# Layer 1 of a two-layer attention trunk: every third pair of probability chunks combined on VectorE, and the sum of squares as two rounded products

## The chip, the cores and the metric

The kernel runs on one core of one Trainium2 chip. The metric is the device time of one execution in microseconds. One execution was also taken by the hardware profiler; where the text speaks of the trace, it means that one.

## The reference

The input x has 2048 tokens of 1024 features. Layer 0 (a sliding-window attention and a chunked one) is not touched by the change. Layer 1 is a differential attention with 8 heads: two softmaxes over the same values, one subtracted from the other, then a norm over each head's 128 features and a gate.

```python
def differential_attention(q1, q2, k1, k2, v, lam):
    ...
        s1 = jnp.einsum('bqhd,bkhd->bhqk', qb1, k1).astype(jnp.float32) * scale
        s2 = jnp.einsum('bqhd,bkhd->bhqk', qb2, k2).astype(jnp.float32) * scale
        p1 = jax.nn.softmax(jnp.where(mask, s1, NEG_INF), axis=-1)
        p2 = jax.nn.softmax(jnp.where(mask, s2, NEG_INF), axis=-1)
        a = p1 - lam * p2
        return jnp.einsum('bhqk,bkhd->bqhd', a.astype(v.dtype), v)
...
    o = differential_attention(q1, q2, k1, k2, v, lam)
    o = rms_norm(o, subln_g) * (1.0 - lambda_init)
    y = (o.reshape(b, s, C_W) * jax.nn.silu(gate)) @ w_out
    return x + y
```

The mask lets a token see its own chunk of 64 tokens and all earlier ones. All of it is in 4-byte floats.

## The kernel before

The kernel runs layer 0, then the projections of layer 1 (q, k, v into DRAM), then the stage `_mix1`, which holds all that the change touches. `_mix1` starts at 1782 us of the span and lasts to the end, 1085 us.

The 2048 queries are cut into four blocks b of 512, each block into four tiles j of 128. The work goes by (head h, block b), 32 of them: first blocks 0 and 1 of each head in turn, then block 2 for all heads, then block 3.

`scores(h, b, ...)` is the first half of one (h, b). For each tile j and each of the two softmaxes m, the visible keys are cut into chunks of up to 512. For a chunk, TensorE multiplies a high and a low part of q with k into a PSUM bank (tile `cS`, L898 and L899), VectorE takes the row's negated maximum (`cnm`, L902), and ScalarE writes the exponentials to SBUF (`cP`, L905) and adds them up. After both softmaxes of a row of chunks, small instructions (L911 to L917) work out the common scale of each chunk: `cpe` at L914 is a VectorE product of two SBUF tiles with at most 8 columns. Then each pair of chunks is made into one, p1 x c1 + p2 x c2. GpSimd scales p1 (L921). For most pairs GpSimd also scales p2 (L930) and adds the two (L931). For every `COMB`th pair VectorE does the second half in one instruction (L928), after a small product for its scalar (L927); both of its inputs lie in SBUF.

`values(h, b, ...)` is the second half. For each 128 keys, TensorE transposes the combined chunks of the four tiles (`ctr`, L944), ScalarE (two in three, L947) or VectorE (one in three, L949) copies the result to SBUF (`cpt`), and TensorE multiplies it with the values into one PSUM bank (`cO`, L951).

`gate(h, b, O)` ends one (h, b). ScalarE copies the sum out of PSUM (`cot`, L966) and squares it (`csq`, L968); the gate's sigmoid is begun (L970, L971) and GpSimd multiplies by the gate (L972). The rest is put off until the third 128 keys of the next (h, b): a product of the squares with a matrix of ones sums over the 128 features (`cms`, L976), in 4-byte operands; ScalarE takes the logarithm (L977), VectorE adds (L978), ScalarE exponentiates (L979), VectorE multiplies (L980). L978 and L980 read two SBUF tiles each. The result goes to DRAM, or is split at once into a high and a low part for the output projection (`split`, L997 and L998).

Beside this, `gates` (the gate's projection, tile `cG`, first) and `projected` (the output projection, tile `com`, later) yield TensorE work in steps of three products (L214 to L216). `pace` runs `heads` (the scores) ahead of the values by `LAG1` units and mixes in the steps of the side work by `STAGES1`. From the program so recorded, a scheduler in the framework sets the final order of each engine's instructions, by its own estimates of their times. All engines run their instructions in that order.

Buffers that the change touches: the pool `pp` holds the chunks of the first softmax until their transposes are done (20 of 512 columns), and `pt` the transposed chunks until their product (6). Operands of the type `F32R` are 4-byte floats that TensorE multiplies in a rounded form. A high part in that type and the difference to the full value as a low part are the kernel's way to keep accuracy; `self.ones` is of that type, and L976 reads it as plain floats.

Of the kernel before, what the change touches and what calls it, by code (L numbers as in the profile page):

```python
# [10 lines left out]
F32 = mybir.dt.float32  # L11
F32R = mybir.dt.float32r
AF = mybir.ActivationFunctionType
ALU = mybir.AluOpType
# [4 lines left out]
P = 128  # L19
# [4 lines left out]
BLK = NTB * P  # L24
# [7 lines left out]
def f32(ap):  # L32
    return ap.bitcast(F32)
# [52 lines left out]
class Trunk:  # L86
# [1 line left out]
    AHEAD = 2  # L88
    BANKS0, LAG0, SHARE0 = (3, 3, 1, 1), 9, 0.85
    FIN = 18  # L90
    COMB = 5
    BANKS1, LAG1 = (4, 2, 1, 1), (30, 30, 36, 36)
    STAGES1 = ((0, 0), (44, 84), (1088, 520))

# [747 lines left out]
    def _mix1(self, es):  # L842
        nc, tc, a, s = self.nc, self.tc, self.a, self.s1
        n = "c"
        pool = lambda nm, bufs, **kw: es.enter_context(tc.tile_pool(name=n + nm, bufs=bufs, **kw))
# [2 lines left out]
        ld = pool("ld", 2)  # L848
        yp = pool("y", 2 * KT)
        vp = pool("v", 4)  # L850
        pp = pool("pp", 20)
        kp = pool("kp", 4)
        sb = pool("sb", 2)
        NS, NTR, NO, NM = self.BANKS1
# [4 lines left out]
        mm = nc.tensor.matmul  # L859
# [17 lines left out]
        def scores(h, b, q, K, res, then):  # L877
# [4 lines left out]
            for j in range(NTB):  # L882
# [35 lines left out]
                for z, (c, ce) in enumerate(cuts):  # L918
# [3 lines left out]
                    count[0] += 1  # L922
                    if count[0] % self.COMB == 0:
                        c2 = rl[:, 1:2]
# [9 lines left out]
        def values(h, b, res):  # L934
            us = res["u"]
            O = pO.tile([P, BLK], F32, tag="O", name=n + "O")
            nkt = (b + 1) * NTB
            for kt in range(nkt):
                j0 = max(0, kt - b * NTB)
                wd = (NTB - j0) * P  # L940
                tp = ptr.tile([P, 512], F32, tag="tr", name=n + "tr")
                kk = (kt % 4) * P
                for j in range(j0, NTB):
                    nc.tensor.transpose(tp[:, (j - j0) * P:(j - j0 + 1) * P], us[j][kt // 4][:, kk:kk + P], self.ident)  # L944
                T = sb.tile([P, 512], F32, tag="pt", name=n + "pt", bufs=6)
                if kt % 3:
                    nc.scalar.activation(T[:, :wd], tp[:, :wd], AF.Copy)  # L947
                else:
                    nc.vector.tensor_copy(T[:, :wd], tp[:, :wd])  # L949
                v = res["v"][kt // 4][:, kk:kk + P]  # L950
                mm(O[:, j0 * P:], v, T[:, :wd], start=(kt == 0), stop=(kt == nkt - 1), skip_group_check=True)  # L951
                if kt == 2:
                    while normal:
                        normal.pop(0)()
                yield wd / P
            gate(h, b, O)
# [3 lines left out]
        def gate(h, b, O):  # L960

            rows, tok = slice(h * P, (h + 1) * P), slice(b * BLK, (b + 1) * BLK)
            g = sb.tile([P, BLK], F32, tag="g", name=n + "gg")
            nc.sync.dma_start(g, s["g"][rows, tok])
            o = ot.tile([P, BLK], F32, tag="ot", name=n + "ot")
            nc.scalar.activation(o, O, AF.Copy)  # L966
            sq = sb.tile([P, BLK], F32, tag="sq", name=n + "sq", bufs=1)
            nc.scalar.activation(sq, o, AF.Square)  # L968
            sg = sb.tile([P, BLK], F32, tag="sg", name=n + "sg", bufs=1)
            nc.scalar.activation(sg, g, AF.Exp, scale=-1.0)  # L970
            nc.scalar.activation(sg, sg, AF.Ln, bias=self.one)  # L971
            nc.gpsimd.tensor_tensor(o, o, g, ALU.mult)  # L972

            def rest():
                ms = ptr.tile([P, BLK], F32, tag="tr", name=n + "ms")
                mm(ms, f32(self.ones), sq, start=True, stop=True)  # L976
                nc.scalar.activation(sq, ms, AF.Ln, bias=self.eps, scale=1.0 / P)  # L977
                nc.vector.scalar_tensor_tensor(sg, sq, 0.5, sg, ALU.mult, ALU.add)  # L978
                nc.scalar.activation(sg, sg, AF.Exp, scale=-1.0)  # L979
                nc.vector.scalar_tensor_tensor(o, o, self.sub, sg, ALU.mult, ALU.mult)  # L980
                if b == 0 or (h, b) in place:
                    split(h, b, o)
                else:
                    nc.sync.dma_start(s["o"][rows, tok], o)
                ended.add((h, b))

            normal.append(rest)
# [7 lines left out]
        def split(h, b, o):  # L995
            yH, yL = y_tiles(h, b)
            nc.scalar.activation(yH, o, AF.Copy)  # L997
            nc.gpsimd.tensor_tensor(yL, o, f32(yH), ALU.subtract)  # L998
            y[b][h] = yH, yL
# [125 lines left out]
        def heads():  # L1125
# [7 lines left out]
            for (h, b), nxt in zip(order, order[1:] + [None]):  # L1133
                at[0] = b
                after, spare = [None, {}], NB - keys(b)
                new = nxt and nxt[0] != h
                if nxt and not new:
                    after[1] = K

                def then(j, m, z):  # L1140
                    if (j, m, z) == (2, 0, 0) and nxt:
                        after[0] = load_q(*nxt)
                    if (j, z) == (1, 0) and new:
                        for i in range(min(spare, keys(nxt[1]))):
                            after[1][i, m] = load_k(nxt[0], i, m)
                    if j == NTB - 1:
                        if new and z + spare < keys(nxt[1]):
                            after[1][z + spare, m] = load_k(nxt[0], z + spare, m)
                        if m == 0 and z not in V:
                            V[z] = load_v(h, z)  # L1150

                res = {}
                yield from scores(h, b, q, K, res, then)
                res["v"] = [V[z] for z in range(b + 1)]
                if new:
                    V = {}
                queue.append(values(h, b, res))
                q, K = after
# [61 lines left out]
```

## Time and profile before

| | before |
|---|---|
| median of 3 runs | 2870.75 us (2856.9 to 2872.15) |
| profiled execution | 2868.88 us, span 2867.1 us |
| mean granted TensorE clock | 0.982 |
| busy in the span: TensorE, VectorE, ScalarE, GpSimd | 2717.2, 1856.3, 1544.8, 1595.3 us |
| busy from 1782 to 2867 us: TensorE, VectorE, ScalarE, GpSimd | 1028.9, 724.6, 688.8, 791.2 us |

In the profile PE is TensorE (PEld its loading of weights), DVE VectorE, ACT ScalarE, POOL GpSimd. A row of a group gives the line, the engine, the operation, the tiles written and read, the shape and the count; then the busy time in us and the mean of one in ns; then the idle time of the engine ahead of these instructions and what ended it. A row of the timeline gives the start and the duration in us, and in brackets the idle time ahead of it and its releaser. Records of TensorE overlap, since its matmuls are pipelined: what one costs in a dense stretch is the step from its start to the next start.

### The profile page before, as it was taken

The page shows a single profiled execution, that of the slowest core. Times are in us where ns is not written, and L with a number is a line of the kernel's source. Part 1 is how long each engine was busy: PE and PEld are TensorE (multiplying, and loading weights), DVE is VectorE, ACT ScalarE, POOL GpSimd, SP SyncE. Part 2 cuts the span into 40 slices and gives each one's busy share as a digit, 9 for nine tenths or more (in the row PEclk, how much of TensorE's full clock was granted, in tenths as well). Part 3 has the DMA queues.
Part 4 walks back from the last instruction along what each step waited for, and adds up shares of the span by engine and source line. Part 5 has one row for each costly group of instructions (what it writes and reads, how often), then busy time and mean ns, then how long its engine had stood idle before and what let it go on. Part 6 is the DMA issues. An engine that isn't in the chain of part 4 may idle for free.

```text
span 2867.1 us, 43943 instructions
## 1 busy us (share of the span) xinstructions
PE 2717.2 (95%) x13384; PEld 2177.3 (76%) x13384; DVE 1856.3 (65%) x4643; ACT 1544.8 (54%) x4015; POOL 1595.3 (56%) x1740
## 2 busy tenths in 40 slices
PE   7999999998899999899999998999999999899999
PEld 5888888787788888777788887776667777566666
DVE  7752285357788875598708860477777677766761
ACT  4443543367767665343344331577777776656652
POOL 3541251334545354267745650578878787878772
PEclk9999999999999999999999999999999999999999
DMA  5673343738877664567875443887858667354543
GB/s 160 226 239 140 114 142 116 232 107 226 229 188 194 181 180 144 191 219 238 264 245 170 132 145 104 268 244 202 235 171 232 180 199 206 112 171 141 149 137 108
DMA packets 356092, 521.68 MB, mean 182 GB/s; under 512 B 44816, under 2 KB 139792, under 8 KB 355856
## 3 DMA queue, kind: packets, MB, share of 16 engines
q1 hardware_dynamic: 355856, 518.87, 60.5%
q8 instruction: 107, 1.75, 0.3%
q14 instruction: 129, 1.06, 0.1%
HBM read 361.70 MB, written 157.02 MB: 181 GB/s over the span
## 4 chain that ended last, share of the span: by engine, by line
PE 71%; DVE 8%; DMA 7%; ACT 4%; issue 2%; POOL 2%; SPq 1%; DVEq 0%; ACTq 0%; POOLq 0%
PE cO L951 7%; PE p1mm L216 5%; PE p1mm L215 5%; PE p1mm L214 5%; PE cS L898 4%; PE cS L899 4%; PE ctr L944 3%; PE p0mm L214 2%; PE p0mm L216 2%; PE p0mm L215 2%; PE com L214 2%; PE com L215 2%; PE com L216 2%; PE mom L214 2%; PE mom L215 2%
## 5 line engine op out<-in xcount | busy, mean ns | idle before, releaser
L905 ACT ACTIVATE cP<-cS,cnm 128x512 f32<-128x512 f32 (+3 forms) x640 | 397.6, 628 | 191.5 <-DVE cnm L902 170.8
L902 DVE TENSOR_REDUCE cnm<-cS 128x1 f32<-128x512 f32 (+3 forms) x640 | 374.3, 603 | 72.4 <-PE cS L899 65.3
L921 POOL TENSOR_SCALAR cP<-cP,crl,ce 128x512 f32<-128x512 f32 (+3 forms) x288 | 215.8, 762 | 186.9 <-DVE crl L916 99.4
L215 PE MATMUL p1mm<-p1wL,p1hH 128*128 128x512 f32 x768 | 302.3, 394 | 0.4 <-POOL p1wL L310 0.4
L214 PE MATMUL p1mm<-p1wH,p1hH 128*128 128x512 f32 x768 | 301.2, 393 | 0.8 <-ACT p1wH L308 0.8
L216 PE MATMUL p1mm<-p1wH,p1hL 128*128 128x512 f32 x768 | 301.9, 393 | 0.0
L951 PE MATMUL cO<-cpt,cv 128*128 128x512 f32 (+3 forms) x640 | 288.6, 539 | 12.3 <-DVE cpt L949 9.6
L310 POOL TENSOR_TENSOR p0wL<-p0ws,p0wH 128x512 fp32r<-128x512 f32 (+1 forms) x124 | 149.7, 1239 | 265.4 <-ACT p0wH L308 255.8
L931 POOL TENSOR_TENSOR cP<-cP,cP 128x512 f32<-128x512 f32 (+3 forms) x256 | 284.9, 1136 | 1.3
L898 PE MATMUL cS<-ck,cqd 128*128 128x512 f32 (+3 forms) x640 | 263.2, 416 | 18.9 <-ACT cP L905 12.0
L310 POOL TENSOR_TENSOR p1wL<-p1ws,p1wH 128x512 fp32r<-128x512 f32 x128 | 169.7, 1346 | 134.3 <-ACT p1wH L308 128.8
L214 PE MATMUL p0mm<-p0wH,p0hH 128*128 128x512 f32 (+1 forms) x640 | 239.1, 375 | 5.2 <-ACT p0vt L472 3.7
L216 PE MATMUL p0mm<-p0wH,p0hL 128*128 128x512 f32 (+1 forms) x640 | 239.5, 375 | 1.5 <-DVE p0hL L336 1.5
L215 PE MATMUL p0mm<-p0wL,p0hH 128*128 128x512 f32 (+1 forms) x640 | 239.1, 374 | 0.0
L899 PE MATMUL cS<-ck,cql 128*128 128x512 f32 (+3 forms) x640 | 234.0, 370 | 4.0 <-DMA cql<-qL 4.0
L944 PEld LDWEIGHTS ctr<-ident,cP 128*128 128x128 f32 x1088 | 137.6, 142 | 115.0 <-issue 60.9
L930 POOL TENSOR_SCALAR cP<-cP,crl,ce 128x512 f32<-128x512 f32 (+3 forms) x230 | 181.4, 800 | 0.7 <-DVE crl L917 0.7
L944 PE MATMUL ctr<-ident,cP 128*128 128x128 f32 x1088 | 174.7, 275 | 2.8 <-POOL cP L931 2.0
L214 PEld LDWEIGHTS p1mm<-p1wH,p1hH 128*128 128x128 f32 x768 | 144.7, 189 | 29.8 <-ACT p1wH L308 1.0
L215 PEld LDWEIGHTS p1mm<-p1wL,p1hH 128*128 128x128 f32 x768 | 144.7, 188 | 29.6 <-POOL p1wL L310 0.8
L216 PEld LDWEIGHTS p1mm<-p1wH,p1hL 128*128 128x128 f32 x768 | 144.7, 188 | 28.7
L898 PEld LDWEIGHTS cS<-ck,cqd 128*128 128x128 f32 x640 | 123.0, 193 | 49.7 <-ACT cP L905 25.6
(306 smaller groups left out, 7296.2 us busy)
## 6 DMA issues: line engine op xcount, KB each, us to landing
p1ws<-in_od_w_in_dram SPq DMA_DIRECT2D x56, 512.0 KB, 4.4
p0ws<-in_ev_w_in_dram SPq DMA_DIRECT2D x48, 512.0 KB, 4.5
ck<-kH SPq DMA_DIRECT2D x144, 128.0 KB, 3.3
ck<-kL SPq DMA_DIRECT2D x144, 128.0 KB, 3.5
cv<-v SPq DMA_DIRECT2D x72, 256.0 KB, 4.2
cqd<-qH SPq DMA_DIRECT2D x128, 128.0 KB, 4.8
cql<-qL SPq DMA_DIRECT2D x128, 128.0 KB, 4.8
cwH<-wgH SPq DMA_DIRECT2D x64, 256.0 KB, 4.6
```

The lines of the kernel that those rows point to most:

```text
L214: mm(ps, aH, bH, start=first, stop=False)
L215: mm(ps, aH, bL, start=False, stop=False)
L216: mm(ps, aL, bH, start=False, stop=last)
L310: low.tensor_tensor(l[:, :width], ws[:, k, :width], f32(h[:, :width]), ALU.subtract)
L898: mm(ps, qd[:, m, js], kt[:, :wd], start=True, stop=False)
L899: self.anchor = mm(ps, ql[:, m, js], kt[:, :wd], start=False, stop=True).ins
L902: nc.vector.tensor_reduce(nm[:, m, z:z + 1], ps, AX.X, ALU.max, negate=True)
L905: nc.scalar.activation(chunks[z][:, :wd], ps, AF.Exp, bias=nm[:, m, z:z + 1], accum_out=acc)
L921: nc.gpsimd.tensor_scalar(p1, p1, rl[:, 0:1], e1, ALU.mult, ALU.mult)
L931: nc.gpsimd.tensor_tensor(p1, p1, p2, ALU.add)
L944: nc.tensor.transpose(tp[:, (j - j0) * P:(j - j0 + 1) * P], us[j][kt // 4][:, kk:kk + P], self.ident)
L951: mm(O[:, j0 * P:], v, T[:, :wd], start=(kt == 0), stop=(kt == nkt - 1), skip_group_check=True)
```

## The change

Three edits. `COMB` goes from 5 to 3, so that VectorE does the second half of every third pair (106 of the 320) and no longer of every fifth (64). The squares are split: ScalarE copies them into the rounded type (`csH`), VectorE subtracts that from the squares (`csL`), and the one product of plain floats becomes two of rounded ones that add up in the same PSUM bank. For the room of the two new tiles `pp` loses one buffer and `pt` one. The lines below L971 move down by up to five: `csH` is at L971, `csL` at L972, the two products are at L980 and L981, and L978, L980 and L1077 of before become L983, L985 and L1082.

```diff
-    COMB = 5
+    COMB = 3
...
-        pp = pool("pp", 20)
+        pp = pool("pp", 19)
...
-                T = sb.tile([P, 512], F32, tag="pt", name=n + "pt", bufs=6)
+                T = sb.tile([P, 512], F32, tag="pt", name=n + "pt", bufs=5)
...
             sq = sb.tile([P, BLK], F32, tag="sq", name=n + "sq", bufs=1)
             nc.scalar.activation(sq, o, AF.Square)
+            sH = sb.tile([P, BLK], F32R, tag="sH", name=n + "sH", bufs=1)
+            sL = sb.tile([P, BLK], F32R, tag="sL", name=n + "sL", bufs=1)
+            nc.scalar.activation(sH, sq, AF.Copy)
+            nc.vector.tensor_tensor(sL, sq, f32(sH), ALU.subtract)
...
             def rest():
                 ms = ptr.tile([P, BLK], F32, tag="tr", name=n + "ms")
-                mm(ms, f32(self.ones), sq, start=True, stop=True)
+                mm(ms, self.ones, sH, start=True, stop=False)
+                mm(ms, self.ones, sL, start=False, stop=True)
```

TensorE's order around the product of the squares of the last (h, b) but one, before and after. The row is the operation, the tiles and the size written.

```order
L951 MATMUL cO<-cpt,cv 128x512 x2
L976 MATMUL cms<-csq,ones 128x512
L951 MATMUL cO<-cpt,cv 128x512
L944 MATMUL ctr<-ident,cP_32130 128x128
L944 MATMUL ctr<-ident,cP_32319 128x128
```

```order
L951 MATMUL cO<-cpt,cv 128x512 x2
L944 MATMUL ctr<-ident,cP_32499 128x128
L944 MATMUL ctr<-ident,cP_32630 128x128
L944 MATMUL ctr<-ident,cP_32775 128x128
L980 MATMUL cms<-csH,ones 128x512
L981 MATMUL cms<-csL,ones 128x512
L951 MATMUL cO<-cpt,cv 128x512
```

The two products stand together, three transposes later than the one did.

VectorE's order in the last row of chunks of the stage, before and after (`cla` and `ce` are the sums and scales of the chunks, `cxr` the residual of the output projection):

```order
L914 TENSOR_TENSOR cpe<-ce,cla 128x8
L915 TENSOR_REDUCE cl<-cpe 128x2
L916 RECIPROCAL crl<-cl 128x2
L917 TENSOR_SCALAR crl<-crl,nlam 128x1
L927 TENSOR_SCALAR cc_33233<-ce,crl 128x1
L928 SCALAR_TENSOR_TENSOR cP_33179<-cP_33212,cc_33233,cP_33179 128x512
L1077 TENSOR_TENSOR cxr<-com,cxr 128x512
L949 COPY cpt<-ctr 128x512
L978 SCALAR_TENSOR_TENSOR csg<-csq,csg 128x512
```

```order
L914 TENSOR_TENSOR cpe<-ce,cla 128x8
L915 TENSOR_REDUCE cl<-cpe 128x2
L916 RECIPROCAL crl<-cl 128x2
L917 TENSOR_SCALAR crl<-crl,nlam 128x1
L927 TENSOR_SCALAR cc_33419<-ce,crl 128x1
L928 SCALAR_TENSOR_TENSOR cP_33351<-cP_33388,cc_33419,cP_33351 128x512
L972 TENSOR_TENSOR csL<-csq,csH 128x512
L1082 TENSOR_TENSOR cxr<-com,cxr 128x512
L949 COPY cpt<-ctr 128x512
L983 SCALAR_TENSOR_TENSOR csg<-csq,csg 128x512
```

The subtraction `csL` comes right behind a combination.

GpSimd's order for one row of four pairs of the last (h, b), before and after:

```order
L921 TENSOR_SCALAR cP_32902<-cP_32902,crl,ce 128x512
L921 TENSOR_SCALAR cP_32922<-cP_32922,crl,ce 128x512
L921 TENSOR_SCALAR cP_32928<-cP_32928,crl,ce 128x512
L921 TENSOR_SCALAR cP_32946<-cP_32946,crl,ce 128x256
L930 TENSOR_SCALAR cP_32955<-cP_32955,crl,ce 128x512
L930 TENSOR_SCALAR cP_32978<-cP_32978,crl,ce 128x512
L930 TENSOR_SCALAR cP_32996<-cP_32996,crl,ce 128x256
L931 TENSOR_TENSOR cP_32902<-cP_32902,cP_32955 128x512
L931 TENSOR_TENSOR cP_32928<-cP_32928,cP_32978 128x512
L931 TENSOR_TENSOR cP_32946<-cP_32946,cP_32996 128x256
```

```order
L921 TENSOR_SCALAR cP_33089<-cP_33089,crl,ce 128x512
L921 TENSOR_SCALAR cP_33109<-cP_33109,crl,ce 128x512
L921 TENSOR_SCALAR cP_33115<-cP_33115,crl,ce 128x512
L921 TENSOR_SCALAR cP_33133<-cP_33133,crl,ce 128x256
L930 TENSOR_SCALAR cP_33159<-cP_33159,crl,ce 128x512
L930 TENSOR_SCALAR cP_33165<-cP_33165,crl,ce 128x512
L931 TENSOR_TENSOR cP_33109<-cP_33109,cP_33159 128x512
L931 TENSOR_TENSOR cP_33115<-cP_33115,cP_33165 128x512
```

Ten instructions became eight: two pairs of this row are now VectorE's, not one.

## The prediction

> **What bounds the kernel now.** I read the totals and the chain on the page first.
>
> ```profile
> PE 2717.2 (95%) x13384; PEld 2177.3 (76%) x13384; DVE 1856.3 (65%) x4643; ACT 1544.8 (54%) x4015; POOL 1595.3 (56%) x1740
> ...
> PE 71%; DVE 8%; DMA 7%; ACT 4%; issue 2%; POOL 2%; SPq 1%; DVEq 0%; ACTq 0%; POOLq 0%
> ```
>
> TensorE carries 71% of the chain that ends last. The edit touches layer 1's attention alone, from 1782 us on, so I cut the busy time by stretch (PE, PEld, DVE, ACT, POOL, then the granted clock):
>
> ```profile
> 1782.00:2867.00 1085.00, 1028.93 (x4608) 754.73 (x4608) 724.59 (x1778) 688.82 (x1928) 791.18 (x896) 0.97 0.63 184
> ...
> 2200.00:2400.00 200.00, 199.89 (x924) 147.14 (x923) 143.88 (x355) 141.68 (x401) 159.75 (x179) 1.00 0.69 201
> 2400.00:2500.00 100.00, 87.09 (x378) 60.66 (x377) 75.37 (x148) 63.67 (x176) 86.19 (x93) 0.93 0.45 127
> 2500.00:2600.00 100.00, 96.40 (x428) 70.35 (x427) 66.04 (x147) 59.13 (x165) 72.55 (x82) 0.98 0.55 166
> 2600.00:2700.00 100.00, 92.51 (x401) 64.94 (x399) 71.44 (x139) 67.01 (x181) 86.92 (x92) 0.97 0.47 137
> 2700.00:2800.00 100.00, 97.50 (x432) 71.38 (x431) 62.24 (x146) 58.17 (x160) 71.88 (x83) 0.97 0.49 150
> ```
>
> In these 1085 us TensorE stands still for 1085 - 1029 = 56 us. The rest of the text is about two things: work taken off TensorE, and whether those 56 us grow or shrink. Who ends them is in TensorE's waits from 1700 us on (us in total, times, longest):
>
> ```profile
> PE cS L898 <- ACT cP L905: 12.0, 10, 3.4
> PE cO L951 <- DVE cpt L949: 9.6, 4, 7.2
> PE com L214 <- DVE cxr L1077: 5.4, 4, 2.1
> PE cG L216 <- DMA cwL<-wgL: 5.0, 1, 5.0
> ...
> PE com L216 <- POOL cy L998: 2.5, 1, 2.5
> PE cO L951 <- ACT cpt L947: 2.3, 1, 2.3
> PE ctr L944 <- POOL cP L931: 2.0, 3, 1.0
> ```
>
> VectorE ends 9.6 + 5.4 us directly. The 12.0 us behind the exponentials are mostly its too, since the exponentials wait for its maxima (first row of the next fence). GpSimd ends only 4.5 us, though it is the busiest of the three helpers.
>
> **The pairs that move from GpSimd to VectorE.** There are 320 pairs of chunks in layer 1: 64 were VectorE's (every fifth), 106 will be (every third), so 42 move.
>
> ```profile
> L905 ACT ACTIVATE cP<-cS,cnm 128x512 f32<-128x512 f32 (+3 forms) x640 | 397.6, 628 | 191.5 <-DVE cnm L902 170.8 <-PE ctr L944 6.4 <-POOL cP L930 5.3
> ...
> L931 POOL TENSOR_TENSOR cP<-cP,cP 128x512 f32<-128x512 f32 (+3 forms) x256 | 284.9, 1136 | 1.3
> ...
> L930 POOL TENSOR_SCALAR cP<-cP,crl,ce 128x512 f32<-128x512 f32 (+3 forms) x230 | 181.4, 800 | 0.7 <-DVE crl L917 0.7
> ...
> L928 DVE SCALAR_TENSOR_TENSOR cP<-cP,cc,cP 128x512 f32<-128x512 f32 (+3 forms) x58 | 63.8, 1100 | 19.1 <-POOL cP L921 18.1 <-DMA cwL<-wgL 0.5
> ...
> L978 DVE SCALAR_TENSOR_TENSOR csg<-csq,csg 128x512 f32<-128x512 f32 x32 | 27.9, 873 | 28.6 <-ACT csq L977 28.4 <-ACT csg L971 0.2
> ...
> L968 ACT ACTIVATE csq<-cot 128x512 f32<-128x512 f32 x32 | 20.4, 639 | 0.1
> ...
> L927 DVE TENSOR_SCALAR cc<-ce,crl 128x1 f32<-128x1 f32 x58 | 12.0, 207 | 1.3
> ```
>
> GpSimd loses 42 x (0.80 + 1.14) = 81 us of 791. VectorE gains 42 x (1.10 + 0.21) = 55 us, and 42 times it also waits for the scaling at L921 (18.1 us over 58, so 0.3 each, 13 us); behind it in VectorE's queue stand the maxima, and behind those the exponentials and the next scores. The saving on GpSimd is off the path: of TensorE's 4.5 us behind it I take back a tenth, 0.5 us (ends: 0 and 4.5).
>
> **The split of the squares.** The copy to sH is a ScalarE pass like the square, 32 x 0.64 = 20 us on top of 689. ScalarE spends 170.8 us before exponentials waiting for VectorE, which covers it; without that cover the 20 us would press on the scores, so its ends are 0 and a few us, and I take 0. The subtraction into sL is a VectorE instruction with two SBUF inputs of 128x512; its nearest row is L978, 0.87 each, 28 us. VectorE thus goes from 725 to 725 + 55 + 28 = 808 us, and its idle share from 33% to 26% (with the 13 us of waiting, 24%).
>
> On TensorE one product of 4-byte operands becomes two rounded ones. Busy times overlap there, so I take steps between starts:
>
> ```profile
> 1841.10 1.02 PE L976 MATMUL cms<-csq,ones 128*128 128x512 f32 x2
> 1841.56 0.80 PE L214 MATMUL cG<-p1hH,cwH 128*128 128x512 f32 x1
> 1842.20 0.40 PE L215 MATMUL cG<-p1hL,cwH 128*128 128x512 f32 x1
> 1842.43 0.39 PE L216 MATMUL cG<-p1hH,cwL 128*128 128x512 f32 x1
> ```
>
> A rounded 512-column product steps by 0.23 (1842.20 to 1842.43). From 1841.10 to 1842.20 stand the old product and one rounded one, so the old one takes 1.10 - 0.23 = 0.87. Two rounded ones take 0.46: 0.41 saved, 32 times, 13.2 us. That is on the engine that bounds; ends: 13.2 where TensorE never waits (2200 to 2400), nothing where the saved time only becomes waiting. TensorE is busy for 95% of the stage: I take 12.5.
>
> At the very end the product itself is waited for:
>
> ```profile
> 2826.21 0.63 ACT L968 ACTIVATE csq<-cot 128x512 f32<-128x512 f32 x1
> ...
> 2826.89 1.13 PE L976 MATMUL cms<-csq,ones 128*128 128x512 f32 x2 [1.35 <-ACT csq L968]
> ...
> 2832.82 1.28 POOL L998 TENSOR_TENSOR cyk<-cot,cyk 128x512 fp32r<-128x512 f32 x1
> ...
> 2836.04 0.39 PE L214 MATMUL com<-p1hH,cyk 128*128 128x512 f32 x1
> ```
>
> TensorE's queue stands for 1.35 us behind the square; now the copy (0.64) comes between: +0.7. The subtraction (0.87) delays the rest of this chain, less 0.41; its last product was ready at 2834.10 for a use at 2836.04, 1.9 us of room, enough for about 1.1 us. Elsewhere the order puts the two products after the transposes of the next block, and I charge nothing; price if a product came too early: its chain is 0.64 + 0.87 = 1.5 us longer, at each of 32 places.
>
> **The smaller pools.** Exponentials wait 6.4 us for a chunk's last transpose (L905's row): one buffer in 20 less, a third of a us. Ends 0 and 6.4, taken as 0. The one buffer less of the transposed chunks takes away waiting room of the copies alone; L947 and L949 stand behind transposes, so 0, at most another 2.3, all that TensorE waits for L947's copies.
>
> **VectorE's longer stalls.** This is the open term.
>
> ```profile
> L914 DVE TENSOR_TENSOR cpe<-ce,cla x96: 144/166/9348, 1802.1 to 2790.8; 128x4 f32<-128x4 f32 x32, 128x6 f32<-128x6 f32 x32, 128x8 f32<-128x8 f32 x32
> ...
> 2475.61 9.35 DVE L914 TENSOR_TENSOR cpe<-ce,cla 128x8 f32<-128x8 f32 x1
> ...
> 2477.54 3.73 POOL L931 TENSOR_TENSOR cP<-cP,cP 128x512 f32<-128x512 f32 x3
> ...
> 2486.76 2.08 PE L951 MATMUL cO<-cpt,cv 128*128 128x512 f32 x2 [7.18 <-DVE cpt L949]
> ...
> 2663.93 7.88 DVE L928 SCALAR_TENSOR_TENSOR cP<-cP,cc,cP 128x256 f32<-128x256 f32 x1
> ...
> 2673.33 0.80 PE L898 MATMUL cS<-ck,cqd 128*128 128x512 f32 x1 [3.17 <-ACT cP L905]
> ```
>
> An 8-column instruction that takes 0.166 in the median took 9.35 us while GpSimd ran back to back, and TensorE stood 7.18 us; a combination took 7.88 and cost 3.17. Both instructions read two SBUF tiles. Such instructions number 96 + 64 + 32 + 32 = 224 now (L914, L928, L978, L980) and 224 + 42 + 32 = 298 then, 1.33 times; GpSimd's load falls to 0.90. Product 1.20: the 10.4 us become 12.4, +2. Ends: -10.4 (no such stall) and +10.4 (twice as many). What else VectorE ends, 9.6 + 5.4 + 12.0 - 10.4 = 16.6 us, I let grow as the inverse of its idle share, 33/26 = 1.27: +4.5; ends 0 and, doubled, +16.6.
>
> The Trainium skill's page "SBUF — State Buffer", section "Who interferes with whom", says that a VectorE instruction with two SBUF inputs and a GpSimd instruction that reads SBUF exclude each other for a whole instruction. By that rule a stall would end with one GpSimd instruction, here 1.3 us, the two long ones would not exist, and the sum would lack its +2. The trace agrees on who collides and not on how long: 9.35 us reach over the three GpSimd additions of the row above and more.
>
> **Sum.** -12.5 - 0.5 + 0.7 + 2 + 4.5 = -5.8 us. The profiled execution took 2868.9 (span 2867.1), 1.9 below the median of 2870.75; 2868.9 - 5.8 = 2863.
>
> **The rivals.** (1) *VectorE's stalls take over: slower.* With 74 more two-source instructions, long stalls that reach TensorE at 7.2 us each: three more (21.6) in place of the +2, and the other waits doubled (16.6 for 4.5) give -5.8 + 19.6 + 12.1 = +26, 2895. It decides from four more stalls of that size on, or two with the waits doubled. For it: VectorE's waits are already the largest group. Against: GpSimd's bursts are shorter; the stall needs a full burst. (2) *GpSimd was the hidden brake: faster.* TensorE idles 12.9 and 7.5 us in the stretches where GpSimd is busy for 86 and 87 of 100, and 3.6 and 2.5 where it is busy for 72. If the two heavy stretches became like the light ones, 14 us come back, beside the 12.5 and without VectorE's terms: -26, 2843. Against: at 2200 to 2400 GpSimd is at 80% and TensorE waits for 0.1. (3) *The saving is swallowed*: the freed 13 us become waiting, 2868.9 + 0.7 + 2 = 2872. In these stretches with waits it may, at 2200 to 2400 it can't.
>
> **How the numbers follow.** A measurement of this kernel can tell about 0.5% (14 us) from no change. My forecast: 0.38; (1) 0.20; (2) 0.30; (3) 0.12. My forecast's own range is 2852 to 2875. Of its 0.38, 0.05 lies below 2856 and 0.01 above 2885; (2) is mostly below (0.27), (1) mostly above (0.17). Faster 0.32, same 0.50, slower 0.18. The range for 8 in 10 reaches from (2)'s 2840 to 2890, inside (1).
>
> **What would show it.** Right: two rounded products per block at steps of 0.23; TensorE's busy time in the stage down by some 8 to 13 us; GpSimd's down by 80; VectorE's up by 80; TensorE's waits for VectorE and the exponentials 3 to 10 us up. Wrong: more VectorE instructions over 5 us with TensorE's waits behind them (1); the 56 us of idle down by 10 or more (2); a wait of TensorE for csL in many blocks.

## The result, and the profile after

The changed kernel takes 2855.0 us in the median of 9 runs (2846.5 to 2862.0), the kernel before 2870.1 in the same session (9 runs, 2856.9 to 2877.0). The ratio is 0.9945 with a 95% interval of 0.9925 to 0.9966: 15 us faster. The forecast was 2863 in a range of 2840 to 2890.

The page after, totals and chain:

```profile
PE 2705.2 (95%) x13384; PEld 2175.9 (76%) x13384; DVE 1890.9 (66%) x4757; ACT 1557.2 (55%) x4047; POOL 1548.9 (54%) x1656
...
PE 67%; DVE 10%; DMA 7%; ACT 4%; POOL 3%; issue 3%; SPq 1%; DVEq 0%; ACTq 0%; POOLq 0%
```

The profiled execution took 2848.2 us, 20.7 less than the one before, but 7.4 of that lie ahead of the stage, in code that didn't change: the stage begins at 1774.6 us, not 1782.0. Over all profiles of this study that start lies between 1774.6 and 1784.3. Two single traces can therefore only be compared stage by stage. The stage after, in the same columns as before:

```profile
1774.60:2846.40 1071.80, 1018.17 (x4608) 754.89 (x4608) 759.50 (x1892) 701.50 (x1960) 747.02 (x812) 0.97 0.64 186
```

It is some 13 us shorter. TensorE's busy time fell by 10.8 us, VectorE's rose by 35, GpSimd's fell by 44. The idle part of TensorE is 53.6 us, before it was 56.1. Its waits have other names now:

```profile
PE cS L898 <- ACT cP L905: 11.9, 14, 2.6
PE cG L214 <- DMA cwH<-wgH: 9.4, 3, 6.8
PE com L214 <- DVE cxr L1082: 4.5, 3, 2.5
PE cO L951 <- DVE cpt L949: 4.4, 7, 1.3
...
PE ctr L944 <- POOL cP L931: 2.7, 3, 1.5
PE cms L980 <- ACT csH L971: 2.4, 2, 2.0
```

The waits for VectorE and for the exponentials fell from 27.0 us to 20.8, with more work on VectorE. Waits for transfers rose in their place. VectorE's two-input instructions after:

```profile
L914 DVE TENSOR_TENSOR cpe<-ce,cla x96: 144/166/2278, 1796.0 to 2768.7; 128x4 f32<-128x4 f32 x32, 128x6 f32<-128x6 f32 x32, 128x8 f32<-128x8 f32 x32
L928 DVE SCALAR_TENSOR_TENSOR cP<-cP,cc,cP x98: 325/984/4887, 1798.0 to 2771.8; 128x512 f32<-128x512 f32 x58, 128x128 f32<-128x128 f32 x18, 128x256 f32<-128x256 f32 x11, 128x384 f32<-128x384 f32 x11
L972 DVE TENSOR_TENSOR csL<-csq,csH x32: 670/732/3176, 1828.1 to 2805.1; 128x512 fp32r<-128x512 f32 x32
```

The longest L914 takes 2.28 us and no longer 9.35.

To compare the experiments, I use three numbers of each trace's stage. *Work*: the steps that TensorE's matmuls need when nothing is waited for, added up (0.226 us for a rounded product of 512 columns, 0.44 for each of the two passes of a plain one, 0.107 for a transpose, narrower ones in proportion). The passes of plain products step by 0.43 in the traces, so 0.44 is a little much: by 0.43 every work would be some 6 us lower, every standing as much higher, and the split would take 13.0 us off the work, not 13.7. *Standing*: the time by which matmuls start later than these steps allow (the expectations call it TensorE's idle time). *Long*: VectorE instructions of over 2 us in the stage that read two SBUF tiles.

Standing is larger than the idle time on the page for two reasons. Overlapping records hide small gaps there. And TensorE's clock is not always granted in full: before, the trace has ten stretches of 3.4 to 13.7 us at half clock in this stage, together 61 us, and each has a wait of TensorE of over 1 us in it or less than 3 us ahead of it. The longest goes with the wait of 7.18 us that the prediction shows. Here are this stretch (the clock is the third number from the end) and, from an undisturbed one, two passes like those that took 2.08 us behind that wait:

```profile
2478.10:2491.70 13.60, 6.42 (x14) 3.05 (x13) 9.19 (x9) 2.23 (x4) 12.75 (x14) 0.50 0.28 77
...
1839.81 1.02 PE L951 MATMUL cO<-cpt,cv 128*128 128x512 f32 x2
```

At half clock a rounded product of 512 columns steps by 0.427 us and not 0.226. TensorE is busy for 45 of the 61 us, so I estimate that 22 us of the standing are slow work and not waiting. A long wait is thus paid twice, and a few long waits more or fewer move TensorE's busy time too.

Before: work 981.4, standing 94.5, long 11. After: work 967.7, standing 94.2, long 4. So by the two profiles the whole gain of the stage is the two rounded products, and nothing else moved. The experiments show that this reading is wrong.

### The profile page after: what moved, and what is told of

Same layout as the page of the kernel before. It is cut to its first block, busy times and chain, and to the rows that moved or that the text cites. A ratio compares the mean times of both kernels' runs of the same rounds, so it can differ in the third digit from the quotient of the medians.

```text
span 2846.4 us, 43958 instructions
## 1 busy us (share of the span) xinstructions
PE 2705.2 (95%) x13384; PEld 2175.9 (76%) x13384; DVE 1890.9 (66%) x4757; ACT 1557.2 (55%) x4047; POOL 1548.9 (54%) x1656
## 4 chain that ended last, share of the span: by engine, by line
PE 67%; DVE 10%; DMA 7%; ACT 4%; POOL 3%; issue 3%; SPq 1%; DVEq 0%; ACTq 0%; POOLq 0%
PE cO L951 7%; PE p1mm L214 4%; PE p1mm L216 4%; PE p1mm L215 4%; PE cS L898 3%; PE ctr L944 3%; PE cS L899 3%; PE p0mm L214 2%; PE p0mm L215 2%; PE p0mm L216 2%; PE mom L214 2%; PE mom L216 2%; PE mom L215 2%; PE com L214 2%; PE com L215 2%
## 5 line engine op out<-in xcount | busy, mean ns | idle before, releaser
L921 POOL TENSOR_SCALAR cP<-cP,crl,ce 128x512 f32<-128x512 f32 (+3 forms) x288 | 221.1, 781 | 207.2 <-DVE crl L916 78.5
L931 POOL TENSOR_TENSOR cP<-cP,cP 128x512 f32<-128x512 f32 (+1 forms) x214 | 254.5, 1208 | 2.0
L930 POOL TENSOR_SCALAR cP<-cP,crl,ce 128x512 f32<-128x512 f32 (+3 forms) x190 | 156.9, 836 | 0.0
```

The costliest lines, as they stand in the source:

```text
L921: nc.gpsimd.tensor_scalar(p1, p1, rl[:, 0:1], e1, ALU.mult, ALU.mult)
L931: nc.gpsimd.tensor_tensor(p1, p1, p2, ALU.add)
```

## The experiments

Each kernel was timed beside the kernel before on the same chip; the ratios are to that. Every edit also changes the order that the scheduler sets. By tiles and sizes, TensorE's order leaves that of before after 35 of 4608 matmuls in the pairs alone, after 615 with L914 on GpSimd, and after 1557 with the smaller pools alone. So an edit can also act through the order, and no run holds the order fixed.

### The two halves of the change apart

The split alone, with its smaller pools, is the changed kernel with one line put back:

```diff
-    COMB = 3
+    COMB = 5
```

> The split of the squares alone (and the smaller pools); every fifth pair stays VectorE's. Theory A (the time follows TensorE's work, the helpers' load is covered): 13 us faster than before, 2857, TensorE's work in the stage down by 13 us and its idle time unchanged. Rival B (part of the gain is GpSimd's relief by the pairs): less than 13, about 2862 to 2866, since VectorE and ScalarE get more work and GpSimd keeps its own. Rival C (the subtraction on VectorE is what helps or harms by stalls): idle time changes by over 5 us.

Measured: 2876.2 us, ratio 1.0035 (1.0021 to 1.0050), 10 us *slower*. Theory A falls, and so does rival B, for neither has a loss; rival C's change of the idle time is there (68.5 us on the page, before 56.1). The work did go down to 967.7, but standing rose to 114.2, with 14 long instructions. VectorE's groups there:

```profile
L914 DVE TENSOR_TENSOR cpe<-ce,cla 128x4 f32<-128x4 f32 (+2 forms) x96 | 61.4, 640 | 33.6 <-ACT ce L913 31.4 <-ACT cP L905 1.8
...
L972 DVE TENSOR_TENSOR csL<-csq,csH 128x512 fp32r<-128x512 f32 x32 | 44.0, 1374 | 9.7 <-ACT csH L971 9.5
```

csL was to take 0.87 us and takes 1.37. Its longest case, from the timeline of VectorE, GpSimd and TensorE in the same kernel:

```profile
2526.59 5.81 DVE L972 TENSOR_TENSOR csL<-csq,csH 128x512 fp32r<-128x512 f32 x1
2532.32 0.15 DVE L914 TENSOR_TENSOR cpe<-ce,cla 128x8 f32<-128x8 f32 x1
...
2527.10 1.29 POOL L931 TENSOR_TENSOR cP<-cP,cP 128x512 f32<-128x512 f32 x1
2528.34 1.30 POOL L976 TENSOR_TENSOR cot<-cot,cgg 128x512 f32<-128x512 f32 x1
2529.59 2.26 POOL L931 TENSOR_TENSOR cP<-cP,cP 128x512 f32<-128x512 f32 x2
2533.08 1.52 POOL L921 TENSOR_SCALAR cP<-cP,crl,ce 128x512 f32<-128x512 f32 x2 [1.23 <-DVE crl L916]
...
2534.03 0.50 PE L214 MATMUL com<-p1hH,cy 128*128 128x512 f32 x1 [2.10 <-DVE cxr L1082]
2543.43 0.50 PE L898 MATMUL cS<-ck,cqd 128*128 128x512 f32 x1 [3.61 <-ACT cP L905]
```

csL starts at 2526.59 while GpSimd runs without a gap, each record beginning before the last one ends, and it ends at 2532.40, just after GpSimd's burst ends at 2531.85. Then GpSimd itself waits 1.23 us for VectorE's scale, and TensorE 2.10 for the residual that stands behind csL. The 3.61 us follow another such stall, a combination of 4.54 us at 2538.08.

The pairs alone are the kernel before with one line of the change:

```diff
-    COMB = 5
+    COMB = 3
```

> Every third pair on VectorE alone; one plain product, the old pools. Theory A: no change, 2870 within 4 us, with 50 us more on VectorE and 75 us less on GpSimd. Rival B (GpSimd was the hidden brake): 8 to 14 us faster, 2856 to 2862, TensorE's idle time in the stage down by that much. Rival D (VectorE's load costs): 5 to 10 us slower, 2875 to 2880.

Measured: 2852.9 us, ratio 0.9957 (0.9941 to 0.9973), 12 us faster with the work unchanged at 981.4. Standing fell to 79.7. Of the long instructions one is left. TensorE's waits for the exponentials and for VectorE's copies are smaller than before (12.0 and 9.6 us), the one for the residual is not (5.4):

```profile
L914 DVE TENSOR_TENSOR cpe<-ce,cla x96: 144/166/2172, 1798.0 to 2769.5; 128x4 f32<-128x4 f32 x32, 128x6 f32<-128x6 f32 x32, 128x8 f32<-128x8 f32 x32
L928 DVE SCALAR_TENSOR_TENSOR cP<-cP,cc,cP x98: 339/1002/1654, 1800.0 to 2771.8; 128x512 f32<-128x512 f32 x58, 128x128 f32<-128x128 f32 x18, 128x256 f32<-128x256 f32 x11, 128x384 f32<-128x384 f32 x11
...
PE cS L898 <- ACT cP L905: 8.4, 10, 2.3
PE com L214 <- DVE cxr L1077: 6.5, 2, 5.1
...
PE cO L951 <- DVE cpt L949: 4.8, 8, 1.1
```

So rival B's size is right. The stage's row tells why VectorE's load didn't cost: it grew by only 6 us (724.6 to 730.4) although 42 combinations came to it, since much of the time that its instructions had stood was gone: L914 took 58.6 us in all before and takes 32.0 here.

```profile
1775.80:2845.80 1070.00, 1025.47 (x4608) 752.86 (x4608) 730.39 (x1860) 688.06 (x1928) 738.08 (x812) 0.98 0.64 186
```

The pools alone, all else as before:

```diff
-        pp = pool("pp", 20)
-                T = sb.tile([P, 512], F32, tag="pt", name=n + "pt", bufs=6)
+        pp = pool("pp", 19)
+                T = sb.tile([P, 512], F32, tag="pt", name=n + "pt", bufs=5)
```

> Only the two pools smaller by one buffer each, all else as before. Theory A: no change, 2870 within 3 us. A rival in which the buffers are what limits the scores' run ahead: 3 to 8 us slower, with more waiting of the exponentials for transposes than the 6.4 us of before.

Measured: 2864.9, ratio 1.0000 (0.9985 to 1.0015). They cost nothing that can be measured. The trace holds a warning, though: here too there are 14 long instructions, 12 of them at L914, which takes 69.9 us in all against 58.6 before, and yet standing is only some 97 us, before it was 94.5. So the number of long instructions alone doesn't set the time; it matters whether TensorE comes to wait behind them. Its order, too, differs from that of before, without a change of the time.

### Is TensorE's work paid in full?

The kernel before with the product over the squares twice:

```diff
-                mm(ms, f32(self.ones), sq, start=True, stop=True)
-                nc.scalar.activation(sq, ms, AF.Ln, bias=self.eps, scale=1.0 / P)
+                mm(ms, f32(self.ones), sq, start=True, stop=False)
+                mm(ms, f32(self.ones), sq, start=False, stop=True)
+                nc.scalar.activation(sq, ms, AF.Ln, bias=self.eps, scale=0.5 / P)
```

> As before, but the plain product over the squares is done twice into the same bank and the sum halved by the scale of the logarithm: 32 times 0.87 us = 28 us more work on TensorE, nothing more on other engines. Theory A: 26 to 28 us slower, 2896 to 2898, TensorE's idle time in the stage unchanged. Rival (freed or added work is swallowed by the waiting): at most half, 2884 or less.

Measured: 2888.3, ratio 1.0078 (1.0061 to 1.0096): 17 to 28 us slower. Work 1009.5, standing 93.0, so 28 us more work. Added work is paid for the most part; "at most half" (1.0049) is excluded. That work which comes off is repaid doesn't follow, and the split alone shows the contrary.

### Which standing, and by whom

Theory L, named in these expectations, says that VectorE instructions with two SBUF inputs are locked out while GpSimd runs back to back, and that TensorE's standing follows; rival G says that GpSimd's load as such is the brake. Three kernels ask which it is. First the product at L914 on GpSimd, all else as before:

```diff
-                    nc.vector.tensor_tensor(pe, e[:, :, :nb], la[:, :, :nb], ALU.mult)
+                    nc.gpsimd.tensor_tensor(pe, e[:, :, :nb], la[:, :, :nb], ALU.mult)
```

> As before, but the small product at L914 (two SBUF tiles of up to 8 columns) is made on GpSimd; nothing else changes. Theory L: VectorE loses the instruction that has the most long stalls (44 us over its 96 undisturbed durations), TensorE's idle time falls by 8 to 15 us, 2851 to 2858. Rival G (GpSimd's load as such is the brake): GpSimd gets 96 more instructions, so no gain or slower, 2866 to 2875.

Measured: 2854.6, ratio 0.9947 (0.9927 to 0.9966), 15 us faster. One moved line, 96 instructions of at most 8 columns, does as much as the whole change. On GpSimd and in the stage:

```profile
L914 POOL TENSOR_TENSOR cpe<-ce,cla 128x4 f32<-128x4 f32 (+2 forms) x96 | 21.3, 222 | 83.8 <-ACT ce L913 83.7
...
1784.20:2852.80 1068.60, 1019.21 (x4608) 747.82 (x4608) 667.60 (x1682) 689.52 (x1928) 809.96 (x992) 0.99 0.65 187
```

GpSimd is busier than before (810 us against 791), VectorE less by 57, long instructions 3, standing 77.9. The half-clock stretches shrink from 61 us to 31, so some 11 of the 16.6 us less standing are, by the same estimate, work that no longer runs slowly. Rival G, that GpSimd's load as such is the brake, falls: here its load went up and the time down.

Then every second pair, all else as before:

```diff
-    COMB = 5
+    COMB = 2
```

> As the pairs alone, but every second pair (160 of 320) on VectorE: 54 more than with every third, about 70 us more on VectorE and 100 us less on GpSimd. Theory L: the long stalls are already gone with every third, so within 5 us of the pairs alone, 2848 to 2858. Rival G: GpSimd's relief goes on paying, 2843 or less. Rival V (VectorE's load takes over): 2860 or more.

Measured: 2851.8, ratio 0.9945 (0.9925 to 0.9966). GpSimd's busy time in the stage is down to 663 us, 75 below the pairs alone, for no measurable gain; one long instruction, standing 85.5. Theory L fits: the long instructions were already gone. But VectorE's busy time rose by 32 us to 762 in this trace, so a gain from GpSimd's relief and a loss from VectorE's load that cancel are not excluded.

Third, in the split alone, VectorE's subtraction replaced by an instruction of one SBUF input:

```diff
-            sL = sb.tile([P, BLK], F32R, tag="sL", name=n + "sL", bufs=1)
-            nc.vector.tensor_tensor(sL, sq, f32(sH), ALU.subtract)
-                mm(ms, self.ones, sL, start=False, stop=True)
+            sL = small("sL")
+            nc.vector.tensor_reduce(sL, f32(sH), AX.X, ALU.max)
+                mm(ms, self.ones, sH, start=False, stop=True)
```

> As the split alone (every fifth pair on VectorE), but VectorE's subtraction of two SBUF tiles is replaced by a maximum over the 512 columns of csH, one SBUF input and about the same length (0.68 us), and the second product reads csH again with the sum halved: the low part of the squares is left out. TensorE, ScalarE and VectorE keep the split's load. Theory L (two-input VectorE instructions are locked out while GpSimd runs back to back, and TensorE's idle time follows): the split alone's idle of 114 us in the stage goes back to 92 to 100, and with 13 us less work the time is 2853 to 2860. Rival W (the added load of VectorE and ScalarE costs by itself): 2870 or more, as the split alone.

Measured: 2865.8, ratio 0.9987 (0.9974 to 1.0001). It is faster than the split alone by 0.0048, about 14 us, but it misses the forecast of 2853 to 2860. The instruction itself no longer stands:

```profile
L972 DVE TENSOR_REDUCE csL<-csH x32: 618/677/687, 1834.0 to 2827.0; 128x1 f32<-128x512 f32 x32
```

Its longest takes 0.687 us, against 5.81. But long instructions are still 14, six of them now at L983, and standing is 107.3: of the 14 to 22 us that theory L wanted off the standing, 7 came. Rival W's 2870 isn't reached either. It isn't isolated to the two inputs alone, for here the second product doesn't wait for VectorE either.

Last, the changed kernel with L914 on GpSimd, by the same line as above:

> The changed kernel with the product at L914 on GpSimd. Theory L: L914's remaining 22 us of standing disappear from VectorE, the stalls of csL and of the combinations stay: 3 to 8 us faster than the changed kernel, about 0.991 of before. Rival G: not faster than the changed kernel.

Measured: 2845.5, ratio 0.9916 (0.9888 to 0.9944), the fastest of all; standing 87.8, long 2. The changed kernel had 0.9945 in its own session, so about 8 us less by the ratios, but the upper end of the one interval lies above the lower end of the other.

### What the split costs

The split alone, csL on GpSimd:

```diff
-            nc.vector.tensor_tensor(sL, sq, f32(sH), ALU.subtract)
+            nc.gpsimd.tensor_tensor(sL, sq, f32(sH), ALU.subtract)
```

> The split alone (every fifth pair on VectorE), with its subtraction csL on GpSimd: 32 x 1.3 = 41 us more on GpSimd, 32 two-input instructions fewer on VectorE. Theory L (standing of two-input instructions is the cost): the split alone was 1.0035 of before; without csL's standing (23 us) and its turn on VectorE it comes to 0.995 to 0.999, TensorE's idle in the stage under 104 us. Rival G (GpSimd's load is the brake): slower than the split alone, 1.005 or more. Rival A2 (ScalarE's extra pass is what costs): stays at 1.0035.

Measured: 2879.8, ratio 1.0041 (1.0024 to 1.0057); theory L's number is missed, and rival A2's, no change against the split alone, is met. With csL on GpSimd its unbroken runs got longer (49 of over 8 us in the stage, 44 in the split alone), and the other instructions stood more: long instructions 24 in place of 14, standing 121.0, L914 74 us in place of 61:

```profile
L914 DVE TENSOR_TENSOR cpe<-ce,cla x96: 145/200/4698, 1798.0 to 2798.0; 128x4 f32<-128x4 f32 x32, 128x6 f32<-128x6 f32 x32, 128x8 f32<-128x8 f32 x32
L972 POOL TENSOR_TENSOR csL<-csq,csH x32: 1266/1280/1738, 1830.7 to 2835.7; 128x512 fp32r<-128x512 f32 x32
```

The remaining three fill a table of the two halves and the place of L914. Their edits are those shown: the split alone with L914 on GpSimd,

> The split alone with the product at L914 on GpSimd, csL on VectorE. Theory L: the split saves TensorE 13 us also without the pairs, if the other two-input instruction is out of the way: 0.991 to 0.994 of before (before with L914 on GpSimd was 0.9947). Rival (the split costs by its load wherever the others stand): 0.996 or more.

the pairs alone with L914 on GpSimd,

> The pairs alone (every third on VectorE), with L914 on GpSimd. Theory L: both remove the same standing, so they don't add up: 0.992 to 0.995 of before, within 4 us of either alone. Rival G: the pairs' relief of GpSimd adds to it, 0.990 or less.

and the changed kernel with both L914 and csL there.

> The changed kernel with L914 and csL on GpSimd. Theory L: only the combinations, L983 and L985 can stand; TensorE's idle under 80 us, 0.988 to 0.991 of before, the fastest so far. Rival G: GpSimd's 41 us more cost, 0.993 or more.

Measured: 2863.8 us, ratio 0.9985 (0.9970 to 1.0000); 2851.3, 0.9937 (0.9921 to 0.9954); 2853.5, 0.9944 (0.9925 to 0.9963). The second is as theory L had it: the pairs and L914's move don't add up. The first and the third miss it, and there the rivals' forecasts came out: 0.996 or more for a split that costs by its load wherever the others stand, 0.993 or more for GpSimd's added 41 us. csL on GpSimd in the last one brought nothing or cost a little.

| ratio to before | L914 on VectorE | L914 on GpSimd |
|---|---|---|
| neither half | 1 | 0.9947 |
| pairs | 0.9957 | 0.9937 |
| split | 1.0035 | 0.9985 |
| both (the change) | 0.9945 | 0.9916 |

| stage | work | standing | long |
|---|---|---|---|
| before | 981.4 | 94.5 | 11 |
| pairs | 981.4 | 79.7 | 1 |
| smaller pools | 981.4 | about 97 | 14 |
| split | 967.7 | 114.2 | 14 |
| both (the change) | 967.7 | 94.2 | 4 |
| L914 on GpSimd | 981.4 | 77.9 | 3 |
| pairs, L914 on GpSimd | 981.4 | 76.3 | 1 |
| split, L914 on GpSimd | 967.7 | 101.4 | 3 |
| both, L914 on GpSimd | 967.7 | 87.8 | 2 |

Against the row that differs by the split and its smaller pools, the split adds 20, 14, 24 and 12 us of standing, and it takes 13.7 off the work. Without the pairs it costs 0.0035 and 0.0038, outside the intervals; with them it gives 0.0012 and 0.0021, inside. So the change's gain is that of the pairs, and the split is about neutral beside them. Put the other way round, the pairs are worth 0.0043 alone and 0.0090 on top of the split: the halves do not add up. Why the split's standing stays even where long stalls are gone isn't settled. By the releasers in the traces, TensorE's standing behind ScalarE grew with the split in all four pairs of rows (24 to 33, 17 to 25, 21 to 25, 20 to 34 us). That could be ScalarE's extra pass, but the smaller pools alone, without that pass, have 31 us there. No run took the pass away alone.

## Why the prediction was near, and which steps failed

The number was 8 us off, and two large errors cancelled in it. That it came so near is luck: the split was forecast as a gain and alone it is a loss, the pairs were forecast as a loss and alone they are the gain.

- *The price of the two products* (0.41 us less, 32 times): right as work, 13 to 14 us. *"That is on the engine that bounds"*, taken at 12.5 us: wrong. Alone the split lost 10 us, since standing grew by 20. Rival (3), which said that the saving would be swallowed and had 0.12, was the nearest for this half.
- *"The saving on GpSimd is off the path"*, 0.5 us, and *+4.5 for VectorE's load*: wrong in sign; both together with the stalls were priced at +6 for the whole change, and the pairs alone gave -12. Rival (2) had the size (-14) and one of its two stretches: with the pairs alone TensorE's idle time from 2400 to 2500 us fell from 12.9 to 6.2, but from 2600 to 2700 only from 7.5 to 6.5. Its agent is not borne out: GpSimd's busy time rose with L914's move while the time fell. The two-input instructions of VectorE that stand behind GpSimd's bursts fit the runs better, but theory L met only four of its eight forecasts.
- *The load of the helpers*: GpSimd's busy time was to fall by 80 us and VectorE's to rise by 80; they fell by 44 and rose by 35. One reason for GpSimd is that the means were taken over all widths: of the 40 combinations that L928's main group gained (58 to 98), only 15 have 512 columns and 14 have 128. On VectorE the standing that left hides part of the load.
- *The waits of TensorE for VectorE and the exponentials*, 3 to 10 us up: they fell by 6.
- *The stalls, 1.33 times the instructions by 0.90 of the load, +2*: the term that failed by its form. Long ones went from 11 to 1 with the pairs and to 4 with the change. I took the chance of standing as proportional to GpSimd's load. The load fell to 0.94, GpSimd's unbroken runs of over 8 us went from 43 to 28 with the pairs and to 31 with the change, and in the row of the order shown two instructions in ten are gone. That the lengths of its runs decide fits these numbers, but no run varied them alone.
- *csL by its nearest row, 0.87*: 0.99 in the change, 1.37 in the split alone.
- *ScalarE's pass costs 0*: not shown, and open, as said below the last table.
- *The end of the kernel, +0.7*: right; TensorE waits 2.01 us there and not 1.35:

```profile
2805.08 0.80 PE L980 MATMUL cms<-csH,ones 128*128 128x512 f32 x1 [2.01 <-ACT csH L971]
```

- *The pools, 0*: right, though the exponentials wait more for transposes:

```profile
L905 ACT ACTIVATE cP<-cS,cnm 128x512 f32<-128x512 f32 (+3 forms) x640 | 398.1, 628 | 202.3 <-DVE cnm L902 161.7 <-PE ctr L944 15.4 <-POOL cP L930 9.1
```

- *Rival (1)*, more stalls, did not happen in the change, but it did in the split alone: with csL added and GpSimd's bursts unshortened, it has 14 long ones and lost 10 us. The smaller pools alone have as many and lost nothing.

## What to carry to other kernels

When one row of a group has a mean several times its median (L914: 0.61 us against 0.166), look at the tail before the busy time: here moving one such tiny instruction to GpSimd gained as much as the whole change. Then check that the bottleneck waits behind it, for a long tail alone need not cost (the smaller pools). Two edits in one change have to be costed, and if possible run, apart; the traces of before and after alone told a clean and wrong story here. Work taken off the busiest engine is a gain only if what replaces it doesn't delay those who feed it.

## What the runs showed of the hardware

A VectorE instruction with two SBUF inputs can stand until GpSimd has run out of queued work, not only for one instruction: 9.35 us for 8 columns before, 5.81 for csL, 8.98 for csL in the fastest kernel. The one of 9.35 us began at 2475.61 and ended at 2484.96. GpSimd ran eight instructions without a gap in that time, the last one until 2484.94, and then waited for VectorE:

```profile
2483.66 1.28 POOL L998 TENSOR_TENSOR cy<-coy,cy 128x512 fp32r<-128x512 f32 x1
2485.79 3.24 POOL L921 TENSOR_SCALAR cP<-cP,crl,ce 128x512 f32<-128x512 f32 x4 [0.85 <-DVE crl L916]
```

All 11 long ones before end 0.02 to 0.55 us behind the end of such an unbroken run. The same instruction of 8 columns took 0.70 us at most on GpSimd itself, and a maximum over 512 columns from one SBUF tile 0.687 at most at the place where the subtraction took up to 5.81. That VectorE lost so much by standing (L914 alone 58.6 us, of which 96 x 0.166 = 16 us would be its undisturbed time) was not to be seen in its busy share of 67%, since standing counts as busy.

Around waits of TensorE the granted clock was 0.50 for 3.4 to 13.7 us at a time, and the steps of its products nearly doubled (0.427 us for 0.226). In a stage of 1085 us that was 61 us before, and 31 with L914 on GpSimd.
